# Gate projections with high and low weight columns side by side, and the decay logits of linear attention as one product over stacked rows

## The chip, the cores and the metric

The kernel runs on one core of a Trainium2 chip (trn2). The number that counts is the device time of one execution, in microseconds, taken as the median of several runs. The engines of the core are named as in the profile: PE is the matrix engine (PEld its weight loads), DVE the vector engine, ACT the scalar engine, POOL the GpSimd engine, and SP the queue that starts nearly all DMA transfers.

## The reference

The kernel computes a two-layer encoder over 512 tokens of width 1024, all in float32. Layer 0 mixes tokens by a bidirectional gated delta rule with eight heads (GDN), layer 1 by bidirectional gated linear attention with four heads (GLA). After each mixer there is a squared-ReLU MLP of width 4096, and after each of the four sublayers a residual addition with layer norm. Cut to what the change touches:

```python
# layer 0: beta and decay of each head, from 32 of the projection's columns
proj = jnp.matmul(h, w_in).astype(F32)
ba = proj[..., A_CONV_CH + A_VW:].reshape(bn, s, 2, 2, A_HEADS)
beta = jax.nn.sigmoid(ba[:, :, 0]).transpose(2, 0, 3, 1)
g = (-jnp.exp(a_log) * jax.nn.softplus(ba[:, :, 1] + dt_bias)).transpose(2, 0, 3, 1)

# layer 1: low-rank forget gate, rank 16 in each of the two directions
proj = jnp.matmul(h, w_in).astype(F32)
gl = proj[..., 2 * B_KW + 2 * B_VW:].reshape(bn, s, 2, B_RANK)
gate_logit = jnp.einsum('bsnr,nrk->nbsk', gl, gate_w2) + gate_b[:, None, None, :]
log_a = (jax.nn.log_sigmoid(gate_logit) / B_TAU)
```

In words: layer 0 multiplies the 512 x 1024 activations by 32 extra weight columns and turns the results into `beta` and `g`. Layer 1 multiplies its activations by 32 extra columns too (16 for each direction), and multiplies each 16-wide result by a 16 x 512 matrix `gate_w2[d]`, which gives 128 decay logits for each token, head and direction.

## The kernel before, in words

**Precision.** A float32 product is made of three products in the type `float32r`. Each operand is split into a high part (a copy into a `float32r` tile, on ACT, line 95) and a low part (the difference, on DVE, line 96). `mm3` (lines 111 to 116) then issues three matmuls that add into one PSUM bank: the stationary operand's high part with the moving one's high part (L114), high with low (L115), and low with high (L116). The activations are kept transposed as `xth` and `xtl` (eight blocks of 128 features, 512 tokens).

**Stages.** The order is GDN, MLP, GLA, MLP. Weights are streamed from HBM: each block lands in a ring of three staging buffers (`wst`), is split, and the halves go into rings of three `wh` and three `wl` buffers (`whl`). A staging buffer is free once both halves were made, and a `wh` buffer once the last matmul that reads it is done.

**The start (GdnConst.gates, lines 1080 to 1160).** Twelve idle transposes, then the transposes of token tiles 0 and 1 (`tp`), then `proj_halves` over two products with the 512 tokens in two halves: `bap` (the 32 gate columns) and `pjk` (the first key block). The transposes of tiles 2 and 3 stand between the first `bap` half and the first `pjk` half. After that `bap` is copied to `yr` (32 x 512, ACT, L1112), transposed in four pieces into `gtp` (L1115), and a chain of some twenty DVE operations on 128 x 64 and 128 x 128 tiles (`gy`, `gd`, `gl`) leads to `gy` (L1142), whose cumulative sums are four small products on PE (`gcp`, L1147 and L1148). These PE instructions keep the order in which they are written.

**The start of GLA (gla, lines 670 to 713).** The 32 gate columns are loaded into `gst`, 16 for each direction with a gap of 16 zero columns between (48 columns, so that the directions lie at partitions 0 and 32 of the result). `proj_halves` makes `gps` (48 x 512), `pjq` and `pjk`. `gps` is split into `glh` and `gll`, and `gate_w2` (two DMAs into `w2f`, with zeros between) into `w2h` and `w2l`.

**The decay logits (GlaHead.gates, lines 756 to 773).** For each of four heads and two directions, `mm3` over the 16 rows of that direction gives a bank `lg`: three matmuls with 16 rows and 512 tokens each. Five ACT operations and one DVE addition turn `lg` into the factors `F`. The two calls of head 0 stand in front of the value projection, those of head h+1 in the levels 16 and 32 of head h (line 733), each just before the `scp` product of that level (L851).

**Order.** Within the GLA heads, PE instructions keep the written order (`in_order`, line 708): `behind(n)` puts n pieces of projection work (`pjv`, `pjq`, `pjk`; six matmuls or so each) between the steps of the attention levels. In the rest of the kernel, and on DVE, ACT and SP everywhere, a list scheduler sets the order from its own estimates, so a change of one instruction can move others.

Of the kernel before, what the change touches and what calls it, by code (L numbers as in the profile page):

```python
# [8 lines left out]
F32 = mybir.dt.float32  # L9
F32R = mybir.dt.float32r  # L10
# [3 lines left out]
ALU = mybir.AluOpType  # L14
# [3 lines left out]
P = 128  # L18
S = 512
D = 1024  # L20
KT = D // P
# [7 lines left out]
class Ctx:  # L29
# [97 lines left out]
    def proj_halves(self, specs, between=None):  # L127


        out = [self.bank([P, S], F32, name=name, tag=tag) for _, name, tag in specs]  # L130
        for hf in range(2):
            sl = slice(hf * 256, hf * 256 + 256)
            for ps, ((wh, wl), _, _) in zip(out, specs):
                n = wh.shape[-1]
                for k in range(KT):
                    self.mm3(ps[:n, sl], wh[:, k, :], wl[:, k, :], self.xth[:, k, sl], self.xtl[:, k, sl],
                             k == 0, k == KT - 1)
                if between:
                    between()
                    between = None  # L140
        return out

# [527 lines left out]
def gla(c, gc, w_in, gate_w2, w_out, ln_g, ln_b, w_next):  # L670
# [3 lines left out]
    tc, nc = c.tc, c.nc  # L674
    H = B_H
    with c.banks(ac=2, tp=2, pj=4), tc.tile_pool(name="gla", bufs=2) as pool:
# [3 lines left out]
        gst = c.wst.tile([P, KT, 48], F32, name="gst", tag="wst")  # L680
        nc.vector.memset(gst, 0.0)
        base = 2 * H * P + 2 * H * B_DV
        for d in range(2):
            c.dma(gst[:, :, 32 * d:32 * d + 16], w_in[:, base + 16 * d:base + 16 * d + 16].rearrange("(k p) n -> p k n", p=P))
        gwh, gwl = c.split(gst, [P, KT, 48])
        specs = [((gwh, gwl), "gps", "ac")]
        specs += [(c.wcols(w_in, c0), nm, "pj") for c0, nm in ((0, "pjq"), (H * P, "pjk"))]
        gps, *qk0 = c.proj_halves(specs)
        glh = pool.tile([48, S], F32R, name="glh", tag="glh", bufs=1)
        gll = pool.tile([48, S], F32R, name="gll", tag="gll", bufs=1)  # L690
        nc.scalar.copy(glh, gps[:48, :])
        nc.vector.tensor_tensor(gll, gps[:48, :], glh.bitcast(F32), ALU.subtract)
        w2f = c.wst.tile([48, S], F32, name="w2f", tag="wst")
        nc.vector.memset(w2f, 0.0)
        for d in range(2):
            c.dma(w2f[32 * d:32 * d + 16, :], gate_w2[d])
        w2h = pool.tile([48, S], F32R, name="w2h", tag="w2h", bufs=1)
        w2l = pool.tile([48, S], F32R, name="w2l", tag="w2l", bufs=1)
        nc.scalar.copy(w2h, w2f)
        nc.vector.tensor_tensor(w2l, w2f, w2h.bitcast(F32), ALU.subtract)  # L700

        par = c.load_ln(ln_g, ln_b, lambda i: pool.tile([P, 512], F32, name=f"ln{i}", bufs=1))
        g = (glh, gll, w2h, w2l, gc.gb, gc.ngb, gc.gcol)
# [42 lines left out]
class GlaHead:  # L746
# [9 lines left out]
    def gates(self, d):  # L756

        c, h = self.c, self.h
        V, A = c.nc.vector, c.nc.scalar
        glh, gll, w2h, w2l, gb, ngb, _ = self.consts  # L760
        if d == 0:
            self.F = self.pool.tile([P, 2, S], F32, name="F", tag="F", bufs=2)
        ps = c.bank([P, S], F32, name="lg", tag="tp")
        rows = slice(32 * d, 32 * d + 16)
        c.mm3(ps, w2h[rows, h * P:(h + 1) * P], w2l[rows, h * P:(h + 1) * P], glh[rows, :], gll[rows, :], True, True)
# [4 lines left out]
        r = self.t2("gr", 1)  # L770
# [198 lines left out]
class GdnConst:  # L969
# [110 lines left out]
    def gates(self, st, k0, bia, coef, cw):  # L1080

        c, pool = self.c, self.pool
        nc = c.nc
        G, V = nc.gpsimd, nc.vector
        M = 4 * A_H
# [6 lines left out]
        V.memset(coef[:, :H2], 1.0)  # L1092
        with c.in_order(mybir.EngineType.PE):
# [5 lines left out]
            with self.then():  # L1099
                st = c.split(st, [P, KT, M])  # L1100
                k0 = c.split(k0, [P, KT, P])
# [9 lines left out]
        yr = pool.tile([M, S], F32, name="yr", tag="E", bufs=2)  # L1111
        nc.scalar.copy(yr, ps[:M, :])  # L1112
        tps = c.bank([P, NT, P], F32, name="gtp", tag="tp")
        for n in range(NT):
            nc.tensor.transpose(tps[:, n, :M], yr[:, n * P:(n + 1) * P], c.ident[:M, :M])  # L1115
# [502 lines left out]
```

## Time and profile before

| what | value |
|---|---|
| median of 3 runs | 1383.04 us (1381.99 to 1383.33) |
| span of the profiled execution | 1383.4 us |
| PE busy | 1353.9 us, 98% of the span, 8361 instructions |
| DVE busy | 1073.9 us, 78% |
| ACT busy | 736.6 us, 53% |
| mean granted clock of PE | 0.996 |

The page gives no other time for the profiled execution than its span, from the first to the last instruction; it lies 0.4 us above the median of the runs. Busy times of different engines overlap. A PE matmul is listed with its whole passage through the array, so the distance between two starts, and not the listed duration, is what one matmul costs in a row of them. "Idle before" names what ended the wait of an engine. In a timeline the columns are start, duration, engine, line, operation, output and inputs, tile sizes and count.

### The profile page before, as it was taken

Reading aid. Unit: us, or ns where it says so; the run is one execution under the profiler, and the core shown is the slowest. Engines: PE = TensorE matmul, PEld = TensorE weight load, DVE = VectorE, ACT = ScalarE, POOL = GpSimd, SP = SyncE. Lnnn points to the kernel's source line nnn. Section 1 sums busy time; section 2 is a strip of 40 time slices with the busy share of each in tenths; the row PEclk is TensorE's granted clock in tenths of the full one; section 3 lists DMA queues with packets and bytes.
Section 4 is the critical chain, followed back from the end, with each engine's and each line's share of the span. In section 5 each row is a group of like instructions: output and inputs, shape, how many; then the busy total and the mean of one; then the engine's idle time right before and its main releaser. Section 6 shows DMA issues by size and latency. Waiting matters only on the chain.

```text
span 1383.4 us, 21226 instructions
## 1 busy us (share of the span) xinstructions
PE 1353.9 (98%) x8361; PEld 1130.9 (82%) x8361; DVE 1073.9 (78%) x1682; ACT 736.6 (53%) x1438; POOL 71.8 (5%) x111
## 2 busy tenths in 40 slices
PE   9999999999999999999999999999999999999997
PEld 8777787777777888888887888888878888888876
DVE  6687787778677997887957587866879787979665
ACT  4676568665743655555543354654446455546440
POOL 4000000000003600000000000000000000000000
PEclk9999999999999999999999999999999999999999
DMA  6221112211251523253132322221225153431141
GB/s 177 74 62 47 46 32 62 52 42 32 79 154 56 172 77 109 74 153 92 47 112 75 96 89 62 61 62 61 87 66 177 52 152 92 122 88 50 46 151 47
DMA packets 146122, 117.11 MB, mean 85 GB/s; under 512 B 7632, under 2 KB 122440, under 8 KB 146024
## 3 DMA queue, kind: packets, MB, share of 16 engines
q1 hardware_dynamic: 144679, 111.57, 27.4%
q0 software_dynamic: 1344, 4.20, 1.1%
q8 instruction: 65, 1.06, 0.3%
q14 instruction: 34, 0.27, 0.1%
HBM read 113.66 MB, written 2.10 MB: 84 GB/s over the span
## 4 chain that ended last, share of the span: by engine, by line
PE 86%; ACT 6%; DVE 5%; DMA 2%; issue 1%; POOL 0%; DVEq 0%; ACTq 0%; POOLq 0%
PE pj L115 5%; PE pj L116 5%; PE pj L114 5%; PE pjv L114 3%; PE pjv L115 3%; PE pX L114 3%; PE pjv L116 3%; PE pX L115 3%; PE pX L116 3%; PE scp L851 2%; PE fxz L114 2%; PE op L1544 2%; PE fxz L115 2%; PE fxz L116 2%; DMA wst<-in_mlp_w 2%; PE pl L115 2%
## 5 line engine op out<-in xcount | busy, mean ns | idle before, releaser
L95 ACT CAST wh<-wst 128x1024 fp32r<-128x1024 f32 x146 | 152.9, 1050 | 221.6 <-PE pj L115 50.7
L96 DVE TENSOR_TENSOR wl<-wst,wh 128x1024 fp32r<-128x1024 f32 x146 | 177.8, 1225 | 73.3 <-ACT wh L95 73.1
L115 PE MATMUL pj<-xtl,wh 128*128 128x512 f32 (+1 forms) x352 | 127.9, 363 | 0.5 <-DVE xtl L163 0.5
L114 PE MATMUL pj<-xth,wh 128*128 128x512 f32 (+1 forms) x352 | 127.4, 363 | 0.8 <-ACT xth L162 0.7
L116 PE MATMUL pj<-xth,wl 128*128 128x512 f32 (+1 forms) x352 | 127.4, 362 | 0.0
L96 DVE TENSOR_TENSOR w2l<-w2r,w2h 128x1024 fp32r<-128x1024 f32 x84 | 102.5, 1223 | 26.3 <-ACT w2h L95 26.3
L95 ACT CAST w2h<-w2r 128x1024 fp32r<-128x1024 f32 x84 | 88.2, 1050 | 63.5 <-PE pX L116 28.1
L115 PEld LDWEIGHTS pj<-xtl,wh 128*128 128x128 f32 x352 | 67.2, 191 | 10.9 <-DVE xtl L163 0.8
L114 PEld LDWEIGHTS pj<-xth,wh 128*128 128x128 f32 x352 | 66.9, 191 | 11.2 <-ACT xth L162 1.2
L116 PEld LDWEIGHTS pj<-xth,wl 128*128 128x128 f32 x352 | 67.1, 191 | 10.2
L115 PE MATMUL pX<-w2l,ah 128*128 128x512 f32 x192 | 75.0, 391 | 0.0
L116 PE MATMUL pX<-w2h,al 128*128 128x512 f32 x192 | 74.9, 390 | 0.0
L114 PE MATMUL pX<-w2h,ah 128*128 128x512 f32 x192 | 74.8, 393 | 0.0
L95 ACT CAST ah<-h 128x1024 fp32r<-128x1024 f32 x46 | 48.4, 1053 | 47.1 <-PE pX L115 19.3
L336 DVE TENSOR_TENSOR w2r<-w2r 128x1024 f32<-128x1024 f32 x48 | 57.5, 1222 | 0.3
L96 DVE TENSOR_TENSOR al<-h,ah 128x1024 fp32r<-128x1024 f32 x46 | 56.3, 1223 | 0.6
L114 PE MATMUL pjv<-wh,xth 128*128 128x512 f32 x128 | 54.8, 428 | 0.0
L116 PE MATMUL pjv<-wh,xtl 128*128 128x512 f32 x128 | 50.2, 392 | 0.0
L115 PE MATMUL pjv<-wl,xth 128*128 128x512 f32 x128 | 50.0, 390 | 0.0
L116 PEld LDWEIGHTS pX<-w2h,al 128*128 128x128 f32 x192 | 36.1, 188 | 7.5
L116 PE MATMUL pjk<-xth,wl 128*128 128x512 f32 (+1 forms) x112 | 41.8, 373 | 0.0
L114 PE MATMUL pjk<-xth,wh 128*128 128x512 f32 (+1 forms) x112 | 41.7, 372 | 0.0
(477 smaller groups left out, 3932.0 us busy)
## 6 DMA issues: line engine op xcount, KB each, us to landing
wst<-in_mlp_w SPq DMA_DIRECT2D x80, 512.0 KB, 4.4
w2r<-in_mlp_w SPq DMA_DIRECT2D x48, 512.0 KB, 3.8
wst<-in_a_w_in SPq DMA_DIRECT2D x32, 512.0 KB, 4.1
wst<-in_b_w_in SPq DMA_DIRECT2D x32, 256.0 KB, 3.0
wst<-in_a_w_out SPq DMA_DIRECT2D x8, 512.0 KB, 3.7
wst<-in_b_w_in SPq DMA_DIRECT2D x8, 512.0 KB, 3.8
wst<-in_b_w_out SPq DMA_DIRECT2D x8, 512.0 KB, 3.5
xt<-in_x SPq DMA_DIRECT2D x4, 512.0 KB, 5.3
```

Source lines behind the costliest of these rows:

```text
L95: nc.scalar.copy(hi, src)
L96: nc.vector.tensor_tensor(lo, src, hi.bitcast(F32), ALU.subtract)
L114: mm(ps, ah, bh, start=start, stop=False, **kw)
L115: mm(ps, ah, bl, start=False, stop=False, **kw)
L116: mm(ps, al, bh, start=False, stop=stop, **kw)
L336: V.tensor_tensor(blocks[a + (q,)], blocks[a + (q,)], blocks[b + (q,)], ALU.add)
L851: T.matmul(ps[:, n, :], kh[:, sl], qh[:, sl], start=True, stop=True)
L1544: T.matmul(op[:, n, :], l, r, start=i == 0, stop=i == len(mm) - 1)
```

## The change

**Weights side by side.** A new helper `side_by_side` makes the two halves of a 32-column weight block in one `wh` buffer of 64 columns: for each group of 16 columns, 16 high columns and then the 16 low ones. In place of one cast and one subtraction there are two of each, on 128 x 8 x 16 elements. `proj_halves` takes such a block (with no `wl`) and issues two matmuls for each block of features in place of three: all 64 columns against the high and against the low activations. The results of high and low columns come out on different partitions and have still to be added.

**The start.** `bap` has 64 rows. `yr` is 64 x 512, and the four transposes become four float32 products with `sum2`, a 64 x 32 matrix of zeros and ones that transposes and adds the two rows of each column. `sum2` is made by one DVE addition from the identity matrix.

**GLA.** `gst` has 32 columns, filled by one DMA without zeros. `gps` has 64 rows: for each direction 16 high and 16 low ones. For each direction one tile `glr[d]` of 96 rows is filled from its 32 rows of `gps`: rows 0 to 31 and 64 to 95 get the high part (two ACT copies), rows 32 to 63 the low part (one DVE subtraction). `w2r[d]` is filled by one DMA that reads `gate_w2[d]` six times, so that 96 rows hold it; ACT casts all 96 to the high part, and DVE puts the low part into rows 64 to 95. The decay logits are then one matmul with 96 rows.

```diff
@@ proj_halves @@
                 for k in range(KT):
+                    if wl is None:
+                        self.nc.tensor.matmul(ps[:n, sl], wh[:, k, :], self.xth[:, k, sl], start=k == 0, stop=False)
+                        self.nc.tensor.matmul(ps[:n, sl], wh[:, k, :], self.xtl[:, k, sl], start=False, stop=k == KT - 1)
+                        continue
                     self.mm3(ps[:n, sl], wh[:, k, :], wl[:, k, :], self.xth[:, k, sl], self.xtl[:, k, sl],
                              k == 0, k == KT - 1)
...
+    def side_by_side(self, st, n):
+
+        nc = self.nc
+        w = self.whl.tile([P, KT, n // 16, 2, 16], F32R, name="wh", tag="wh")
+        v = st.rearrange("p k (d r) -> p k d r", r=16)
+        for d in range(n // 16):
+            nc.scalar.copy(w[:, :, d, 0, :], v[:, :, d, :])
+        for d in range(n // 16):
+            nc.vector.tensor_tensor(w[:, :, d, 1, :], v[:, :, d, :], w[:, :, d, 0, :].bitcast(F32), ALU.subtract)
+        return w.rearrange("p k d s r -> p k (d s r)"), None
@@ gla @@
-        gst = c.wst.tile([P, KT, 48], F32, name="gst", tag="wst")
-        nc.vector.memset(gst, 0.0)
+        gst = c.wst.tile([P, KT, 32], F32, name="gst", tag="wst")
         base = 2 * H * P + 2 * H * B_DV
-        for d in range(2):
-            c.dma(gst[:, :, 32 * d:32 * d + 16], w_in[:, base + 16 * d:base + 16 * d + 16].rearrange("(k p) n -> p k n", p=P))
-        gwh, gwl = c.split(gst, [P, KT, 48])
-        specs = [((gwh, gwl), "gps", "ac")]
+        c.dma(gst, w_in[:, base:base + 32].rearrange("(k p) n -> p k n", p=P))
+        specs = [(c.side_by_side(gst, 32), "gps", "ac")]
...
-        glh = pool.tile([48, S], F32R, name="glh", tag="glh", bufs=1)
-        gll = pool.tile([48, S], F32R, name="gll", tag="gll", bufs=1)
-        nc.scalar.copy(glh, gps[:48, :])
-        nc.vector.tensor_tensor(gll, gps[:48, :], glh.bitcast(F32), ALU.subtract)
-        w2f = c.wst.tile([48, S], F32, name="w2f", tag="wst")
-        nc.vector.memset(w2f, 0.0)
+        R = slice(0, 32), slice(32, 64), slice(64, 96)
+        glr, w2r = [], []
         for d in range(2):
-            c.dma(w2f[32 * d:32 * d + 16, :], gate_w2[d])
-        w2h = pool.tile([48, S], F32R, name="w2h", tag="w2h", bufs=1)
-        w2l = pool.tile([48, S], F32R, name="w2l", tag="w2l", bufs=1)
-        nc.scalar.copy(w2h, w2f)
-        nc.vector.tensor_tensor(w2l, w2f, w2h.bitcast(F32), ALU.subtract)
+            w2f = c.wst.tile([96, S], F32, name="w2f", tag="wst")
+            src = gate_w2[d]
+            c.dma(w2f, bass.AP(src.tensor, src.offset, [[0, 6]] + [list(q) for q in src.ap]))
+            t = pool.tile([96, S], F32R, name=f"w2r{d}", bufs=1)
+            nc.scalar.copy(t, w2f)
+            nc.vector.tensor_tensor(t[R[2], :], w2f[R[2], :], t[R[2], :].bitcast(F32), ALU.subtract)
+            w2r.append(t)
+            g = pool.tile([96, S], F32R, name=f"glr{d}", bufs=1)
+            nc.scalar.copy(g[R[0], :], gps[R[d], :])
+            nc.scalar.copy(g[R[2], :], gps[R[d], :])
+            nc.vector.tensor_tensor(g[R[1], :], gps[R[d], :], g[R[0], :].bitcast(F32), ALU.subtract)
+            glr.append(g)
@@ GlaHead.gates @@
-        rows = slice(32 * d, 32 * d + 16)
-        c.mm3(ps, w2h[rows, h * P:(h + 1) * P], w2l[rows, h * P:(h + 1) * P], glh[rows, :], gll[rows, :], True, True)
+        c.nc.tensor.matmul(ps, w2r[d][:, h * P:(h + 1) * P], glr[d], start=True, stop=True)
@@ GdnConst.gates @@
         V.memset(coef[:, :H2], 1.0)
+        self.sum2 = pool.tile([2 * M, M], F32, name="sum2", bufs=1)
+        iv = c.ident[:2 * M, :2 * M].rearrange("p (d s r) -> p d s r", s=2, r=16)
+        V.tensor_tensor(self.sum2.rearrange("p (d r) -> p d r", r=16), iv[:, :, 0, :], iv[:, :, 1, :], ALU.add)
...
-                st = c.split(st, [P, KT, M])
+                st = c.side_by_side(st, M)
...
-        yr = pool.tile([M, S], F32, name="yr", tag="E", bufs=2)
-        nc.scalar.copy(yr, ps[:M, :])
+        yr = pool.tile([2 * M, S], F32, name="yr", tag="E", bufs=2)
+        nc.scalar.copy(yr, ps[:2 * M, :])
         tps = c.bank([P, NT, P], F32, name="gtp", tag="tp")
         for n in range(NT):
-            nc.tensor.transpose(tps[:, n, :M], yr[:, n * P:(n + 1) * P], c.ident[:M, :M])
+            nc.tensor.matmul(tps[:, n, :M], yr[:, n * P:(n + 1) * P], self.sum2, start=True, stop=True)
```

**What moves.** Built, the changed kernel keeps the order of PE but for the matmuls that are gone and for one step: the eight transposes of token tile 2 at the end of the first MLP stand together some eight matmuls earlier than before. On DVE the mask copies of the levels (L885, L887) stand one or two places earlier in each head, some weight subtractions (L96) too, and near the end of the first MLP a clearing of 48 x 512 elements and a weight subtraction are gone from ahead of the last two operations (L216) of tile 2's layer norm. On SP there is one DMA fewer, and the two of `w2f` take two staging buffers where they took one.

More of the change, by code (lines that the diff above doesn't have):

```diff
@@ L702, in gla @@
         par = c.load_ln(ln_g, ln_b, lambda i: pool.tile([P, 512], F32, name=f"ln{i}", bufs=1))
-        g = (glh, gll, w2h, w2l, gc.gb, gc.ngb, gc.gcol)
+        g = (glr, w2r, gc.gb, gc.ngb, gc.gcol)
         heads = [GlaHead(c, pool, h, w_in, g, gc.masks, oth, otl) for h in range(H)]
@@ L759, in gates @@
         V, A = c.nc.vector, c.nc.scalar
-        glh, gll, w2h, w2l, gb, ngb, _ = self.consts
+        glr, w2r, gb, ngb, _ = self.consts
         if d == 0:
```

## The prediction

> **What bounds the kernel now.** I read the page's busy shares first, then the chain of work that ended last, then PE's waits in the two stretches that the diff touches.
>
> ```profile
> PE 1353.9 (98%) x8361; PEld 1130.9 (82%) x8361; DVE 1073.9 (78%) x1682; ACT 736.6 (53%) x1438; POOL 71.8 (5%) x111
> ...
> PE 86%; ACT 6%; DVE 5%; DMA 2%; issue 1%; POOL 0%; DVEq 0%; ACTq 0%; POOLq 0%
> ```
>
> PE is busy for 98% of the span and carries 86% of the chain, so a matmul that goes is worth its step on PE unless a wait takes its place. The waits of PE from 0 to 60 us, from 720 to 960 us, and one stage by engines (duration, then busy time of PE, PEld, DVE, ACT and POOL, granted clock, DMA share, GB/s):
>
> ```profile
> PE gcp L1147 <- DVE gy L1142: 2.3, 1, 2.3
> ...
> PE pjq L114 <- DVE xt L449: 0.9, 1, 0.9
> ...
> 795.00:830.00 35.00, 35.00 (x178) 29.03 (x175) 28.40 (x46) 20.11 (x33) 0.00 (x0) 1.00 0.30 90
> ```
>
> In the GLA heads PE never waits, and DVE works 28.40 of 35 us. At the start PE waits 2.3 us for the chain of gate operations on DVE, so there the end of that chain, not PE, sets the time.
>
> **Six decay-logit calls (heads 1 to 3).** One call with its neighbours, and for comparison a level without such a call:
>
> ```profile
> 824.37 0.39 PE L116 MATMUL pjq<-xth,wl 128*128 128x512 f32 x1
> 824.68 0.50 PE L114 MATMUL lg<-glh,w2h 16*128 16x512 f32 x1
> 825.03 0.40 PE L115 MATMUL lg<-gll,w2h 16*128 16x512 f32 x1
> ...
> 825.59 1.16 PE L851 MATMUL scp<-qh,kh 128*128 128x128 f32 x8
> ...
> 826.82 0.39 PE L115 MATMUL pjq<-xtl,wh 128*128 128x512 f32 x1
> ```
>
> ```profile
> 814.38 0.40 PE L116 MATMUL pjv<-wh,xtl 128*128 128x512 f32 x1
> 814.61 1.05 PE L851 MATMUL scp<-qh,kh 128*128 128x128 f32 x8
> ...
> 815.74 0.40 PE L115 MATMUL pjv<-wl,xth 128*128 128x512 f32 x1
> ```
>
> From the last matmul before to the second one after, the call's stretch takes 826.82 - 824.37 = 2.45 us, the other 815.74 - 814.38 = 1.36 us. Three matmuls of a usual step of 0.23 us (814.38 to 814.61) would be 0.69 us; the call costs 1.09 us. The rest is at the borders: the first `lg` comes after 0.31 us, takes 0.35 us until the next, and from `scp` to the second matmul behind it pass 1.23 us, not 1.13; the third `lg` is left late too. The operand of 16 rows (16*128) is the only thing that differs there. The new matmul has 96 rows, and the built program places it on the array as the 128-row ones; I take it at a usual step of 0.23 us with no border. Gain 1.09 - 0.23 = 0.86 us, six times 5.2 us. From below: if 96 rows have the same borders, the stretch is 0.31 + 0.35 + 1.23 = 1.89 us, and the gain 0.56 us, six times 3.4 us. I take the upper end, as the placing is that of the neighbours.
>
> The Trainium skill ("TensorE: Matmul & The Clock Gate", Part 3, "The mechanism") says that a weight load overlaps running matmuls only where its row group differs. The trace doesn't bear it out in this form: PEld is busy for 29.03 of 35 us under a PE that never waits, nearly all of it loads of 128 rows under matmuls of 128 rows. By that rule 96 rows, which share row groups with 128, would keep the border; that is the first rival below.
>
> **The pair of calls of head 0.**
>
> ```profile
> 794.19 0.28 PE L116 MATMUL pjk<-xth,wl 128*128 128x256 f32 x1
> 794.40 0.50 PE L114 MATMUL lg<-glh,w2h 16*128 16x512 f32 x2
> ...
> 795.30 0.50 PE L114 MATMUL pjv<-wh,xth 128*128 128x512 f32 x1
> 795.63 0.39 PE L115 MATMUL pjv<-wl,xth 128*128 128x512 f32 x1
> ```
>
> Here each row counts two matmuls, one of each direction: the six take 795.30 - 794.40 = 0.90 us, as the three of one call did (825.59 - 824.68 = 0.91 us). The two directions lie on different rows of the array and run side by side, which the change gives up. So the gain is less than twice 0.86 us: 1.44 us (794.19 to 795.63) become 0.12 + 3 x 0.23 = 0.81 us, gain 0.6 us, or with borders 0.21 + 0.35 + 0.23 + 0.33 = 1.12 us, gain 0.3 us.
>
> **The gate columns of GLA (`gps`), and what its products wait for.**
>
> ```profile
> L114 PE MATMUL gps<-xth,wh x16: 276/276/321, 783.2 to 788.3; 128*48 128x256 f32 x16
> ...
> L116 PE MATMUL gps<-xth,wl x16: 276/276/279, 783.4 to 788.6; 128*48 128x256 f32 x16
> ```
>
> The 48 matmuls start between 783.2 and 788.6 us, a step of 5.4 / 47 = 0.115 us. Sixteen go: 1.8 us, all on PE's path, since PE waits for nothing behind them. A load of 64 columns in place of 48 stays under that step. What could be late is the stacked operand of the first `lg`:
>
> ```profile
> 788.76 1.05 ACT L95 CAST wh<-wst 128x1024 fp32r<-128x1024 f32 x1 [6.59 <-PE gps L115]
> 789.71 0.58 ACT L691 CAST glh<-gps 48x512 fp32r<-48x512 f32 x1
> ```
>
> ACT is released by `gps` at 788.76, after the change 1.8 us earlier at 786.9. Then stand two copies of 0.58, the cast of 1.05 and two more copies: 790.3. DVE's last `glr` part follows the 1.2 us subtraction of that cast: about 791.0, estimated. PE reaches `lg` at 794.40 - 1.8 = 792.6, so 1.6 us are left, and the longer chain (three more copies, one more subtraction) costs nothing; without that cover it would cost the excess over 1.6 us once. The two `w2f` DMAs (six times the rows) go out on SP before the `pjv` weights, where before there stood two as well; I cost them at nothing, as they are covered by the 12 us until ACT reads them:
>
> ```profile
> L50 SPq DMA_DIRECT2D w2f<-in_b_gate_w x2: 332/372/413, 767.8 to 768.1; - x2
> ...
> L699 ACT CAST w2h<-w2f x1: 620/620/620, 780.6 to 780.6; 48x512 fp32r<-48x512 f32 x1
> ```
>
> **The moved transposes at the end of the first MLP: a loss.**
>
> ```profile
> 767.21 0.48 DVE L694 MEMSET w2f<- 48x512 f32 x1
> ...
> 767.63 1.21 DVE L96 TENSOR_TENSOR wl<-wst,wh 128x1024 fp32r<-128x1024 f32 x1
> 768.77 1.40 DVE L216 SCALAR_TENSOR_TENSOR xt<-xt,rstd,ln 128x512 f32<-128x512 f32 x2
> ...
> 769.65 0.63 PE L159 MATMUL tp<-ident,xt 128*128 128x128 f32 x4
> ```
>
> The transposes of tile 2 move seven or eight matmuls of 0.23 us forward, to 768.0. DVE's last layer-norm operations lose the clearing and the subtraction ahead of them (768.77 - 767.21 = 1.56 us) but gain about 0.25 us for the second `gst` cast and subtraction: they run from 767.45, end at 768.15 and 768.85, and with the 0.18 us from 769.47 to 769.65 the two groups of four can start at 768.33 and 769.03. PE waits 0.3 and 0.35 us there, less 0.1 us for one change of kind fewer: +0.5 us, between 0 and 0.8.
>
> **The start.**
>
> ```profile
> L114 PE MATMUL bap<-xth,wh x16: 276/276/306, 8.1 to 18.7; 128*32 128x256 f32 x16
> ...
> L116 PE MATMUL bap<-xth,wl x16: 276/276/306, 9.1 to 18.9; 128*32 128x256 f32 x16
> L95 ACT CAST wh<-bst x1: 418/418/418, 7.7 to 7.7; 128x256 fp32r<-128x256 f32 x1
> L95 ACT CAST wh<-gst x1: 513/513/513, 764.7 to 764.7; 128x384 fp32r<-128x384 f32 x1
> 21.95 1.05 ACT L95 CAST wh<-wst 128x1024 fp32r<-128x1024 f32 x1 [1.35 <-PE pjk L115]
> 22.07 0.43 PE L1115 MATMUL gtp<-ident,yr 32*128 32x32 f32 x4
> 22.43 0.50 PE L114 MATMUL pjq<-xth,wh 128*128 128x512 f32 x1
> 23.04 1.32 DVE L96 TENSOR_TENSOR wl<-wst,wh 128x1024 fp32r<-128x1024 f32 x1
> 39.04 0.38 PE L1147 MATMUL gcp<-gy,cum 128*128 128x32 f32 x2 [2.26 <-DVE gy L1142]
> 39.93 0.48 PE L116 MATMUL pjz<-xth,wl 128*128 128x512 f32 x1
> ```
>
> Each half of `bap` loses 8 matmuls. In the second half that is 8 x 0.115 = 0.9 us. In the first, two matmuls now run before the low part is there, and 22 from 9.1 us on: until 11.6. Afterwards all 16 need both parts. A cast of 256 elements takes 418 ns and one of 384 takes 513, so one of 128 some 320 ns, and two 0.23 us more than the one; the subtractions follow behind. I put the start at 9.25 us (9.1 to 9.5) and the end at 9.25 + 16 x 0.115 = 11.1: gain 0.5 us. Four transposes (0.36 us, 22.07 to 22.43) become four float32 products; the nearest row is `gcp`, four such of 32 columns in 39.93 - 39.04 = 0.89 us: +0.5 us. PE is 1.4 us earlier at `gtp` and 0.9 us after it. The DVE chain starts with `gtp` and with the subtraction at 23.04, which waits for the cast at 21.95 and so for `pjk`; they come 0.9 and 1.4 us earlier. I take 1.2 us for the chain's end, and so for the gain, as PE still waits at `gcp` (0.6 to 1.6). The other new instruction, `sum2`, stands on an idle DVE.
>
> **Sum.** -5.2 - 0.6 - 1.8 + 0.5 - 1.2 = -8.3 us against the profiled 1383.4 us, which is 0.4 us over the median of 1383.04. From the median: 1374.7 us.
>
> **Rivals.** First, the borders stay with 96 rows: gains 3.4 and 0.3 in place of 5.2 and 0.6, so 1376.8 us. For it speaks that a row count other than 128 had borders, against it the placing.
>
> Second, the clock drops at the start. After the wait at `gcp` the trace has this stretch (same columns, PE only):
>
> ```profile
> 40.20:43.70 3.50, 3.50 (x10) 0.52 0.36 108
> ```
>
> A wait of 2.26 us and 0.9 us of small products were followed by 3.5 us at half clock, a loss of 1.7 us. The gap of PE ahead of the first `bap` is broken now at 8.1 us; without these two matmuls it lasts some 2.1 us, nearly as long. Then 1374.7 + 1.7 = 1376.4 us; were the drop after `gcp` to go instead, 1373.0. The Trainium skill ("TensorE: Matmul & The Clock Gate", Part 1, "What's actually happening") puts the drop after an idle window of about 3.4 us, free-running. The trace agrees on the 3.4 us at half clock, not on the idle time needed. By the page neither gap would drop the clock.
>
> Third, DVE becomes the bound in the heads: with 28.40 of 35 us busy its share rises as PE shortens, and the six calls' 5.2 us come back as waits: 1379.9 us, and within 0.2% if the pair's and half of `gps`'s go too. PE's lack of any wait there speaks against it.
>
> Fourth, slower: DVE stands earlier in line for the mask copies (L887). If it blocks there until `scp` is done, the E, F, kh and qh work behind it starts late, and the next `scp` waits for kh, with PE's order fixed:
>
> ```profile
> 821.92 0.68 DVE L865 TENSOR_TENSOR kh<-k,E 128x512 f32<-128x512 f32 x1
> ```
>
> A place costs F, kh, qh and a subtraction, 3 x 0.68 + 1.22 = 3.3 us, four heads 13 us: 1388 us. It decides from the point where DVE's lead is gone. This kh is ready at 822.6, 3.0 us ahead of the `scp` at 825.59, and longer ahead of its own one; so I hold it unlikely.
>
> **How the numbers follow.** Forecast 0.60 (own range 1373.5 to 1376.2), borders 0.17, clock 0.10, DVE bound 0.09, slower 0.04. A change under 0.2% (2.8 us) can't be told from none in this kernel; of the DVE rival I count 0.05 as faster and 0.04 as the same. Faster 0.92, same 0.04, slower 0.04. The range goes from 1373.0 (the drop after `gcp` gone) to 1378.5 (borders and a lost 1.7 us), which leaves out the last two rivals.
>
> **What would show it.** `lg` steps of 0.23 us and `scp` 0.23 us behind them confirm 5.2; 0.35 us shows the borders. `gps` should take 3.7 us for 32 starts. `gcp` should start near 37.8 us, `tp` of tile 2 should show waits on L216 of 0.3 us, and the first `bap` start at 9.25. A wait of `lg` on `glr`, of `scp` on kh, or half clock near 10 us would make the prediction wrong.

## The result, and the profile after

The changed kernel takes 1374.01 us in the median of four runs (1370.78 to 1376.46), beside 1383.18 us for the kernel before: ratio 0.9928, 95% interval 0.9913 to 0.9943. Measured once more it was 1373.43 us (six runs) against 1383.12 us: ratio 0.9935, 0.9915 to 0.9955. The forecast was 1374.7 us, with a range from 1373.0 to 1378.5 us. The profiled execution took 1370.78 us, its span is 1369.1 us. That one is 3.2 us faster than the median. In all runs here the span is 1.6 to 2.0 us shorter than the time of its execution, so the profiled execution of before, with its span of 1383.4 us, took about 1385 us, some 2 us over its median and not 0.4. The two spans must not be compared without asking which part of the difference is the change.

The busy shares and the chain of waits of the kernel after:

```profile
PE 1341.5 (98%) x8317; PEld 1123.9 (82%) x8317; DVE 1073.9 (78%) x1685; ACT 738.7 (54%) x1444; POOL 72.5 (5%) x111
...
PE 83%; ACT 7%; DVE 6%; DMA 2%; issue 1%; POOL 0%; DVEq 0%; SPq 0%; ACTq 0%
```

PE is still the bound. It has 44 matmuls fewer; DVE's busy time is the same as before, ACT's 2.1 us longer. PE's waits from 0 to 60 us and from 720 to 960 us (total, times, longest), and the stage that answers to the one from 795 to 830 us:

```profile
PE bap L137 <- DVE wh L155: 2.0, 1, 2.0
...
PE gcp L1164 <- DVE gy L1159: 1.3, 1, 1.3
...
PE scp L865 <- DVE qh L876: 0.7, 1, 0.7
...
789.00:824.00 35.00, 34.33 (x177) 28.98 (x176) 28.90 (x48) 20.76 (x35) 0.00 (x0) 1.00 0.31 90
```

Two things are new: a wait of 2.0 us ahead of `bap`, where before there stood 1.03 and 0.54 us with two matmuls between them, and a wait of 0.67 us of one `scp` in the GLA heads, where PE had waited for nothing. The wait at `gcp` fell from 2.3 to 1.3 us.

**The places of the change.** One decay-logit call with its neighbours, and the pair of head 0 (here one row counts both directions):

```profile
823.18 0.40 PE L116 MATMUL pjk<-xth,wl 128*128 128x512 f32 x1
823.42 0.39 PE L779 MATMUL lg<-glr,w2r 96*128 96x512 f32 x1
823.65 1.05 PE L865 MATMUL scp<-qh,kh 128*128 128x128 f32 x8
...
824.78 0.39 PE L115 MATMUL pjk<-xtl,wh 128*128 128x512 f32 x1
```

```profile
787.46 0.28 PE L116 MATMUL pjk<-xth,wl 128*128 128x256 f32 x1
787.58 0.63 PE L779 MATMUL lg<-glr,w2r 96*128 96x512 f32 x2
...
788.29 0.40 PE L115 MATMUL pjv<-wl,xth 128*128 128x512 f32 x1
```

The stretch takes 824.78 - 823.18 = 1.60 us where it took 2.45: 0.85 us gained, with steps of 0.24 and 0.23 us on both sides of `lg`. The pair takes 788.29 - 787.46 = 0.83 us where it took 1.44: 0.61 us gained. The gate columns, the start, and the moved transposes:

```profile
L137 PE MATMUL gps<-xth,wh x16: 276/276/331, 778.2 to 781.7; 128*64 128x256 f32 x16
L138 PE MATMUL gps<-xtl,wh x16: 276/276/280, 778.4 to 781.8; 128*64 128x256 f32 x16
```

```profile
8.97 0.33 PE L137 MATMUL bap<-xth,wh 128*64 128x256 f32 x1 [2.02 <-DVE wh L155]
...
20.36 1.07 PE L1132 MATMUL gtp<-sum,yr 64*128 64x32 f32 x8
21.37 0.50 PE L114 MATMUL pjq<-xth,wh 128*128 128x512 f32 x1
...
37.05 0.38 PE L1164 MATMUL gcp<-gy,cum 128*128 128x32 f32 x2 [1.34 <-DVE gy L1159]
...
762.59 0.39 PE L116 MATMUL pl<-w2h,w2r 128*128 128x512 f32 x1
762.84 1.29 PE L174 MATMUL tp<-ident,xt 128*128 128x128 f32 x8
```

I compared the starts of PE's matmuls in both traces, in order, and noted where their distance changes:

| place | forecast, us | from trace to trace, us |
|---|---|---|
| start, up to `gcp` | -1.2 | -2.0 (39.04 to 37.05), up to 0.5 of it not the change |
| moved transposes of tile 2 | +0.5 | +0.2, and no wait shown |
| `gps` | -1.8 | -1.7 |
| pair of head 0 | -0.6 | -0.6 |
| `scp` of head 0, second level | none | +0.95 (0.67 us of wait, the rest a border) |
| six calls | -5.2 | -5.1 |
| sum | -8.3 | -8.25 |

Up to 0.5 us of the first row is where the clock rose. In every trace here PE runs at half clock until the first boundary that its clock record shows: ahead of it the transposes follow each other by 0.21 us, behind it, where any are left, by 0.11. In the trace of before it lies at 6.17 us, in that of the changed kernel at 5.09. The kernel with the GLA part alone (below) starts like the one before, and its boundary lies at 4.91 us: its `gcp` starts at 38.55 us, 0.49 us earlier than before with nothing changed ahead of it. Against that trace the changed start gains 1.5 us.

The spans differ by 14.3 us, 6 us more than the sum. Of these, 3.1 us come from the clock: the profiled execution of before spent two periods of 3.41 us at half clock (from 40.31 and from 436.25 us), that of after none. Another 2.4 us were lost near 1331 us by the profiled execution of before alone, where PE waited for late weights:

```profile
PE pl L114 <- ACT w2r L95: 1.4, 1, 1.4
```

None of the other eleven traces of this study has this wait, those with the start or the GLA heads of before among them, so it does not belong to the change. The half clock from 436.25 us comes and goes too: four of the twelve traces have it, among them three with both parts of the change. Whether the one right behind `gcp` is partly the change's is not shown: both traces with the start of before have it, and five of the eight with the changed start and `gcp` in its old place. The change is thus worth 7.8 to 8.3 us in this pair of traces; the medians are 9.2 and 9.7 us apart, with intervals of 8 to 12 and 6 to 12 us.

### The profile page after: what moved, and what is told of

Its sections match the earlier page's. It is cut to its first block, busy times and chain, and to the rows that moved or that the text cites. A ratio compares the mean times of both kernels' runs of the same rounds, so it can differ in the third digit from the quotient of the medians.

```text
span 1369.1 us, 21146 instructions
## 1 busy us (share of the span) xinstructions
PE 1341.5 (98%) x8317; PEld 1123.9 (82%) x8317; DVE 1073.9 (78%) x1685; ACT 738.7 (54%) x1444; POOL 72.5 (5%) x111
## 3 DMA queue, kind: packets, MB, share of 16 engines
q8 instruction: 65, 1.06, 0.3%
## 4 chain that ended last, share of the span: by engine, by line
PE 83%; ACT 7%; DVE 6%; DMA 2%; issue 1%; POOL 0%; DVEq 0%; SPq 0%; ACTq 0%
PE pj L115 5%; PE pj L116 5%; PE pj L114 5%; PE pX L114 3%; PE pX L115 3%; PE pX L116 3%; PE pjv L114 3%; PE pjv L115 3%; PE pjv L116 3%; PE fxz L114 2%; PE scp L865 2%; PE op L1561 2%; PE fxz L115 2%; PE fxz L116 2%; PE pl L115 2%; PE pl L116 2%
## 5 line engine op out<-in xcount | busy, mean ns | idle before, releaser
L96 DVE TENSOR_TENSOR wl<-wst,wh 128x1024 fp32r<-128x1024 f32 x146 | 178.9, 1232 | 62.2 <-ACT wh L95 62.1
L96 DVE TENSOR_TENSOR w2l<-w2r,w2h 128x1024 fp32r<-128x1024 f32 x84 | 102.5, 1222 | 26.6 <-ACT w2h L95 26.5
L96 DVE TENSOR_TENSOR al<-h,ah 128x1024 fp32r<-128x1024 f32 x46 | 56.2, 1221 | 0.6
L114 PEld LDWEIGHTS pX<-w2h,ah 128*128 128x128 f32 x192 | 35.8, 188 | 7.1 <-ACT w2h L95 0.3
```

Of the source, the lines that this page charges most:

```text
L96: nc.vector.tensor_tensor(lo, src, hi.bitcast(F32), ALU.subtract)
L114: mm(ps, ah, bh, start=start, stop=False, **kw)
```

## The experiments

The open questions were whether the six calls' price lies where the forecast put it, what the start is worth once the clock has its say (its gap ahead of `bap` is longer now), and where the new wait of `scp` comes from.

### The start alone, and the GLA part alone

Each kernel takes one part of the diff and leaves the other as before. The first keeps `side_by_side` for `bap`, and `sum2`; the second keeps it for `gps`, and the 96-row product. The first, against the changed kernel:

```diff
-        specs = [(c.side_by_side(gst, 32), "gps", "ac")]
+        gwh, gwl = c.split(gst, [P, KT, 48])
+        specs = [((gwh, gwl), "gps", "ac")]
...
-        c.nc.tensor.matmul(ps, w2r[d][:, h * P:(h + 1) * P], glr[d], start=True, stop=True)
+        c.mm3(ps, w2h[rows, h * P:(h + 1) * P], w2l[rows, h * P:(h + 1) * P], glh[rows, :], gll[rows, :], True, True)
```

> The kernel before with the start alone changed (bap side by side, sum2). Theory, that the gain is the earlier end of the gate chain: gcp starts near 37.05 us as in the changed kernel (39.04 before), all later steps keep their distance, so 2.0 us less: about 1381.2 us; 1.6 us less again where the half clock after gcp stays away. Rival, that the start gives nothing once the clock and the landing of weights are taken out: gcp back at 39 us and 1383.

Measured: 1381.93 us (ten runs) against 1382.51 us, ratio 0.9994 (0.9983 to 1.0005). In its trace `gcp` comes 1.5 us earlier than before, though its clock rose late, at 7.43 us, but the median gains only 0.6 us. The mean granted clock over the ten runs was 0.9953, and 0.9969 over the thirteen runs of the kernel before beside them; 0.0016 of 1380 us is 2.2 us. So the start's gain is real on PE's path, and the clock can have taken most of it. This is argued from means: the one trace of this kernel has no half clock between its start and its last microseconds, and over all 33 runs of the kernel before that list a clock, the mean is 0.9963, not 0.9969.

The second kernel, against the changed one:

```diff
-                st = c.side_by_side(st, M)
+                st = c.split(st, [P, KT, M])
...
-            nc.tensor.matmul(tps[:, n, :M], yr[:, n * P:(n + 1) * P], self.sum2, start=True, stop=True)
+            nc.tensor.transpose(tps[:, n, :M], yr[:, n * P:(n + 1) * P], c.ident[:M, :M])
```

> The kernel before with the GLA part alone changed. Theory: gps 1.7 us less, the pair 0.6 less, six calls 5.1 less, the new wait of scp on qh in head 0 0.9 more: 6.5 us less, about 1376.7 us, whatever the clock does at the start. Rival, that part of the measured gain is the clock alone: the ledger of the starts on PE inside GLA shows under 5 us.

Measured: 1376.04 us (four runs), ratio 0.9952 (0.9934 to 0.9970), 6.5 us less than before. The starts of its matmuls show `gps` -1.7, pair -0.6, `scp` +0.9 and six calls -5.1 us, which is the -6.5 that was expected; the moved transposes, left out there, add 0.2. The gains of the two parts, 0.6 and 6.5 us, come to 7.1 us and not to the 9 us of the whole change; their intervals (0.7 us lost to 2.3 gained for the start, 4 to 9 gained for GLA) are wide enough for the difference.

### Three products in each call, and an operand of 32 rows

If a call before cost two steps of 0.23 us and the borders of a 16-row operand, then three 96-row products should cost two steps more and no border, and one 32-row product a border and no step. The first kernel writes the same product three times into the bank:

```diff
         c.nc.tensor.matmul(ps, w2r[d][:, h * P:(h + 1) * P], glr[d], start=True, stop=True)
+        c.nc.tensor.matmul(ps, w2r[d][:, h * P:(h + 1) * P], glr[d], start=True, stop=True)
+        c.nc.tensor.matmul(ps, w2r[d][:, h * P:(h + 1) * P], glr[d], start=True, stop=True)
```

> The changed kernel with each decay-logit matmul issued three times over 96 rows (the same product again, so the count is that of before, and the result is the same). Theory, that the old call cost three steps and borders, and that 96 rows have no border: a call costs two steps of 0.23 us more than in the changed kernel, 0.46 us, six calls 2.8 us and the pair 0.9. Rival, that the border belongs to three matmuls in a row into one bank: 0.8 us or more a call, 5 us for six.

```profile
821.29 0.40 PE L116 MATMUL pjq<-xth,wl 128*128 128x512 f32 x1
821.52 0.39 PE L779 MATMUL lg<-glr,w2r 96*128 96x512 f32 x1
...
821.99 0.40 PE L781 MATMUL lg<-glr,w2r 96*128 96x512 f32 x1
822.23 1.05 PE L867 MATMUL scp<-qh,kh 128*128 128x128 f32 x8
```

Every step is 0.23 or 0.24 us, and the six calls cost 0.48 us each more than in the changed kernel, the pair 0.9 us. The other kernel leaves out two of the three products, those with the low part of the gate activations and with the low part of `gate_w2`:

```diff
-        c.nc.tensor.matmul(ps, w2r[d][:, h * P:(h + 1) * P], glr[d], start=True, stop=True)
+        c.nc.tensor.matmul(ps, w2r[d][0:32, h * P:(h + 1) * P], glr[d][0:32, :], start=True, stop=True)
```

> The changed kernel with the decay-logit matmul over the first 32 of its 96 rows: the low part of the gate activations and of gate_w2 is left out of the logits. Still one matmul a call. Theory, that the border comes with an operand of fewer than 65 rows or so: the border is back, 0.3 us a call more than with 96 rows, six calls 1.8 us. Rival, that the number of rows does nothing: starts on PE as in the changed kernel within 0.1 us a call.

```profile
822.11 0.39 PE L116 MATMUL pjq<-xth,wl 128*128 128x512 f32 x1
822.43 0.50 PE L779 MATMUL lg<-glr,w2r 32*128 32x512 f32 x1
822.85 1.16 PE L865 MATMUL scp<-qh,kh 128*128 128x128 f32 x8
...
824.08 0.39 PE L115 MATMUL pjq<-xtl,wh 128*128 128x512 f32 x1
```

One product of a third of the rows costs more than one of 96: 0.32 us until it starts and 0.42 us until `scp`, then 1.23 us, together 1.97 us where the changed kernel takes 1.60. From trace to trace each of the six calls costs 0.38 us more. So 0.48 us for two steps and 0.38 us for the border make up the 0.86 us of the forecast, each shown by itself (the border with one product of 32 rows, where the kernel before had three of 16). Where between 32 and 96 rows the border begins, no run shows. The single times (1376.66 and 1377.06 us, one run each) hold half-clock periods and say less than the steps.

The Trainium skill ("TensorE: Matmul & The Clock Gate", Part 3, "The mechanism") has a weight load overlap running matmuls only where its row group differs. These runs don't agree: 96 rows share row groups with the 128-row neighbours and lose nothing, 32 rows lose 0.38 us.

### When the clock drops

The trace records periods of 3.413 us with one clock each. They don't start with the program: the first recorded boundary lay 4.91 to 7.65 us after its first instruction, in another place in each execution. Seven traced executions have the changed start without the ten transposes that follow below. In four of them PE ran at half clock right behind the first `bap`, in three it didn't. Two of them, the changed kernel when measured again and the start alone, with the period that holds the wait and the one behind it (duration, then busy time of PE, PEld, DVE, ACT, POOL, granted clock, DMA share, GB/s):

```profile
7.12:10.53 3.41, 1.56 (x14) 1.33 (x13) 3.04 (x6) 2.41 (x5) 0.00 (x0) 1.00 0.96 345
10.53:13.95 3.42, 3.42 (x19) 3.42 (x18) 0.53 (x2) 0.63 (x2) 0.00 (x0) 0.50 0.71 194
```

```profile
7.43:10.84 3.41, 1.61 (x14) 1.37 (x13) 3.00 (x6) 2.26 (x5) 0.00 (x0) 1.00 0.89 323
10.84:14.26 3.42, 3.42 (x32) 3.42 (x31) 1.70 (x4) 2.16 (x5) 0.00 (x0) 1.00 0.80 219
```

Much the same wait (1.85 and 1.80 us) lay 0.1 us differently in its period: 1.56 us of busy PE were followed by half clock, 1.61 us were not. Over all executions with this start, 1.54 to 1.59 us of work in the period led to half clock (four times), 1.61 us and more to full clock (three times). Around `gcp` there is a boundary too, but elsewhere: up to 2.13 us half clock, 2.17 us and more full clock. At a third place, from 427 to 437 us, periods with up to 1.86 us of work were followed by half clock (four traces), those with 2.06 us and more were not (eight). So the busy time as the profile counts it is not quite what the clock goes by, but within each of the three places it separates every case. In the profile of the changed kernel all three fell on the good side; the start:

```profile
5.09:8.50 3.41, 1.81 (x15) 1.34 (x13) 2.47 (x5) 2.70 (x7) 1.29 (x3) 1.00 1.15 311
```

The Trainium skill ("TensorE: Matmul & The Clock Gate", Part 1, "What's actually happening") describes windows of 3413 ns that run free of the program, and the traces agree. It asks for an idle window before the clock drops, and here the traces differ: 1.56 of 3.41 us, 46% of PE's time, were busy in the first row above, and the clock dropped.

If this is the cause, breaking the gap up should keep the clock:

```diff
             xposes((0, 1), ("ac", "ch", "tp"))
+            for i in range(10):
+                nc.tensor.transpose(idle[:, i % NT, :], c.ident, c.ident)
```

> The changed kernel with ten transposes of the identity (about 0.06 us each) put on TensorE between the transposes of tiles 0 and 1 and the first `bap` product, so that the wait of 1.8 to 2.1 us ahead of `bap` is broken up; nothing of the result changes. Theory (the clock halves for one period of 3.41 us in those executions in which a period falls well on that wait, as at 10.63 us of the kernel with three lg products and at 8.65 us of the one with 32 rows): no half clock near 8 to 14 us, the first `bap` no later than 9.0 to 9.3 us, and the median 1 to 2 us under that of the changed kernel, about 1372.5, ratio 0.992. Rival (the drop at the start has another cause, or is a drop that comes elsewhere later anyway): median that of the changed kernel, about 1374 us, ratio 0.993 to 0.994, and half clock still to be seen in other places as often as before.

```profile
5.16:8.57 3.41, 2.82 (x24) 2.34 (x22) 2.56 (x5) 2.71 (x7) 1.22 (x3) 1.00 1.17 304
```

The period now holds 2.82 us of work, the ten transposes taking 0.11 us each and not 0.06. The clock did what the theory says: none of the three kernels with these transposes has half clock at the start, and over their 15 runs the mean granted clock was 0.9971, against 0.9955 over the 24 runs of all kernels with the changed start and no transposes. The time didn't follow: 1375.58 us (five runs), ratio 0.9945 (0.9927 to 0.9963), not the expected 1372.5. At the same clock as the profiled changed kernel the profiled execution is 1.2 us longer, and the starts of the matmuls put that at one place, at 983 us, where an `stp` product waits for a copy on ACT (0.9 us) that stands behind a weight cast whose data landed late. All three kernels with the transposes have that wait, but so has the GLA part alone, whose start is that of before. Whether the transposes have to do with it stays open.

### The wait of `scp` for qh

In the trace after, this is the place (PE, then ACT, then DVE):

```profile
801.74 1.13 PE L865 MATMUL scp<-qh,kh 128*128 128x128 f32 x8 [0.67 <-DVE qh L876]
```

```profile
794.51 1.04 ACT L95 CAST wh<-wst 128x1024 fp32r<-128x1024 f32 x1
795.44 0.64 ACT L783 ACTIVATE ge<-ge 128x512 f32<-128x512 f32 x1
...
797.44 0.63 ACT L787 ACTIVATE F<-gr 128x512 f32<-128x512 f32 x1 [1.36 <-DVE gr L786]
```

```profile
795.58 1.23 DVE L96 TENSOR_TENSOR wl<-wst,wh 128x1024 fp32r<-128x1024 f32 x1 [2.11 <-ACT wh L95]
...
800.91 0.68 DVE L876 TENSOR_TENSOR qh<-q,F 128x512 f32<-128x512 f32 x1
```

Before, ACT had this order:

```profile
801.37 0.63 ACT L769 ACTIVATE ge<-ge 128x512 f32<-128x512 f32 x1
801.91 1.03 ACT L95 CAST wh<-wst 128x1024 fp32r<-128x1024 f32 x1
802.85 0.63 ACT L773 ACTIVATE F<-gr 128x512 f32<-128x512 f32 x1
```

A weight cast now stands ahead of the last `ge`, between two activations that stood together before. Before, it followed that `ge` and lay over DVE's addition to `gr`, for which F has to wait anyway. Now the addition waits for the later `ge` and stands behind the cast's subtraction on DVE (795.58) as well: from the first `ge` of the pair to F pass 797.44 - 793.99 = 3.45 us, before 802.85 - 800.71 = 2.14. So F is 1.3 us later, and with it the E, F, kh and qh work on DVE. One kernel puts that cast, and its subtraction, behind F:

```diff
-        A.activation(self.F[:, 1 - d, :], r, AF.Exp, scale=-1.0 / 16.0)
+        self.gate = A.activation(self.F[:, 1 - d, :], r, AF.Exp, scale=-1.0 / 16.0)
...
-            wh, wl = c.split(st, [P, 2, 2 * B_DV])
+            with c.tc.issue_after(self.gate.ins) if h == 0 and q == 3 else contextlib.nullcontext():
+                wh, wl = c.split(st, [P, 2, 2 * B_DV])
```

> The changed kernel with the last weight cast of head 0 (the split ahead of `vr`, fourth quarter) held back until the exponential that makes F of the second level has been issued on ScalarE. Theory (the wait of 0.67 us of the first `scp` of the second level for `qh` comes from one ScalarE cast of weights that slipped ahead of `ge` when the logits came earlier): that wait is gone, `scp` starts 0.7 to 0.95 us earlier against the products before it than in the changed kernel, and nothing else moves by over 0.2 us. Rival (VectorE is late there by itself): the wait stays at 0.5 us or more, or goes over to kh or to the products of the fourth quarter.

```profile
804.59 1.06 PE L866 MATMUL scp<-q,ge 128*128 128x128 f32 x8
805.49 1.16 PE L866 MATMUL scp<-qh,kh 128*128 128x128 f32 x8
```

The wait is gone: `scp` follows 0.90 us behind the product before it, not 1.73, and all matmuls behind it come 0.95 us earlier against the changed kernel; nothing else in the GLA heads moves. The cause is the place of this weight split, its cast on ACT and its subtraction on DVE together; the run does not separate the two. The run took 1374.51 us, with three periods at half clock.

### The products over `gy` later, and the edits together

The remaining wait at `gcp` should go if its products stand seven matmuls later in PE's order:

```diff
...
+                    m = c.mm3(ps, wh[:, k, :], wl[:, k, :], c.xth[:, k, :], c.xtl[:, k, :], k == 0, k == KT - 1)
+                    if h == 0 and i == 3 and k == 6:
+                        for s in g.sums:
+                            c.tc.add_manual_dep(s.ins, m.ins.name, mybir.DependencyInfo(
+                                mybir.DependencyClass.NoSync, mybir.DependencyReason.DATA), reason="later")
```

> The changed kernel with the four products over `gy` (lines 1164 and 1165) put seven products of k, v or q later in TensorE's order, so that TensorE no longer waits for VectorE's `gy` there. Theory (the wait of 1.3 us at `gcp` is a plain loss of the start, left over from the 2.3 us of before, and it also gives the clock an occasion to drop): the wait is under 0.2 us, the work behind `gcp` starts about 1.3 us earlier, no half clock between 37 and 47 us; 1.3 us less than the changed kernel at like clock, up to 3 us less where that had dropped. Rival (VectorE is the bound through the first linear attention head and what is gained at `gcp` is waited for again at the first levels): the gain is under 0.4 us from 60 us on.

```profile
PE gcp L1165 <- DVE gy L1159: 0.4, 1, 0.4
```

The wait fell to 0.4 us and PE was 0.8 us better off at 45 us, counted from the first `bap`, which came 0.75 us later in this execution. But the scheduler then set another order for the first GDN heads, new waits of 0.3 us appeared there, and by 425 us 1.5 us had been lost again. One run: 1374.90 us. This is no gain. The three edits together:

> The changed kernel with the three edits of the kernels of this call together: ten transposes ahead of the first `bap`, the weight cast behind F, the products over `gy` seven products later. Theory: the gains add, -0.9 (scp) -1.3 (gcp) -1 to -2 (clock at the start and behind gcp): median about 1370.5 us, ratio 0.991, against about 1374 of the changed kernel. Rival (the scheduler gives part of it back, or the clock's drops move elsewhere): 1372.5 to 1374.

Measured: 1373.16 us (five runs), ratio 0.9932 (0.9916 to 0.9948). The theory's 1370.5 us is missed: of the three gains, that of `scp` came (-0.92 us in the trace) and the clock's (mean 0.9978), the one at `gcp` was given back in the heads, and the `stp` wait took 0.9 us. Without that edit:

> The changed kernel with two of the three edits: ten transposes ahead of the first `bap`, and the weight cast behind F; the products over `gy` stay where the changed kernel has them, because their later place lost 1.5 us in the heads between 60 and 435 us. Theory: against the changed kernel, run beside it on the same chip, 0.95 us less from `scp` and a clock that is higher by 0.001 to 0.002 (1.4 to 2.8 us of time): 2.3 to 3.7 us less, median near 1371.5 where the changed kernel has 1374 to 1375. Rival (transposes that fill the wait only move the drop elsewhere): 0.9 us less at most, mean clock as in the changed kernel.

> The changed kernel itself, unedited, beside the version with two edits and the kernel before on one chip. Theory: ratio 0.993 to 0.9945 to before, mean clock over its runs 0.9955, below the 0.997 of the two kernels with the ten transposes, since the wait ahead of `bap` drops the clock in about half of the executions. Rival: mean clock 0.997, as with the transposes.

Measured on one chip: 1372.51 us (five runs, mean clock 0.9966) for the two edits, 1373.43 us (six runs, 0.9953) for the changed kernel, 1383.12 us for before. The trace of the first shows the `scp` wait gone, but PE waits 1.9 us at `gcp`, 0.6 us longer than in the changed kernel (the reason stands below, at the start), and 0.6 us at `stp`. The version with the two edits is 0.9 us faster in the median, not the 2.3 to 3.7 us of its theory, and its interval (0.9918 to 0.9943) does not separate it from the changed kernel (0.9915 to 0.9955). The ratio and the clock expected for the changed kernel came true. A better kernel than the changed one is thus not shown, and the clock's drops are only part of what spreads its runs.

## Why the prediction was right, and where it was not

The forecast lay 0.7 us over the first median and 1.3 us over the second, and the sum of its steps agrees with the traces to 0.05 us. That closeness is in part luck: three errors cancel, and up to 0.5 us of the measured sum is not the change.

**Six calls, pair, `gps`: right, with their reasons.** 5.1, 0.6 and 1.7 us against 5.2, 0.6 and 1.8. The choice between 96 rows with and without a border, which carried 1.8 us, was made by the placing; the products of 32 and of three times 96 rows confirm it. The first rival (borders stay) is out. `glr` was ready in time, as said: `lg` waits for nothing. That a load of 64 columns stays under the 0.115 us step of `gps` holds for the step, which is 0.116 us after; the load itself is listed with 0.13 us.

**The start: mis-sized, 1.2 where the traces have 1.5 to 2.0.** Two bounds in it were off but small: `bap` starts at 8.97 and not 9.25 us, and the four products cost 21.37 - 20.36 = 1.01 us in place of 0.36, so 0.65 more and not 0.5. The step that failed is "they come 0.9 and 1.4 us earlier. I take 1.2 us for the chain's end". The chain's parts did come 1.06 and 1.29 us earlier, but the chain itself also became shorter, and that wasn't looked for. DVE and POOL, before:

```profile
24.28 1.31 DVE L1131 TENSOR_SCALAR gd<-ge 128x128 f32<-128x128 f32 x1
...
27.08 1.14 DVE L1133 TENSOR_TENSOR ge<-ge,gd 128x128 f32<-128x128 f32 x1
```

```profile
23.44 2.07 POOL L1059 TENSOR_TENSOR off<-blk 128x512 f16<-128x512 f32 x1
...
26.78 1.29 POOL L1059 TENSOR_TENSOR off<-blk 128x512 f16<-128x512 f32 x1
```

And after:

```profile
21.75 2.35 DVE L96 TENSOR_TENSOR wl<-wst,wh 128x1024 fp32r<-128x1024 f32 x1
24.03 0.36 DVE L1148 TENSOR_SCALAR gd<-ge 128x128 f32<-128x128 f32 x1
...
25.86 0.37 DVE L1150 TENSOR_TENSOR ge<-ge,gd 128x128 f32<-128x128 f32 x1
```

```profile
21.73 1.29 POOL L1073 TENSOR_TENSOR off<-blk 128x512 f16<-128x512 f32 x1
```

The same two operations take 1.31 and 1.14 us where they meet POOL's TENSOR_TENSOR, and 0.36 and 0.37 us where they don't. Before, both met it; after, POOL starts first, the weight subtraction meets it (2.35 us, not 1.32), and both operations are free: 0.95 + 0.77 - 1.03 = 0.69 us, which is what 1.29 lacks to 2.0. Against the GLA part alone, whose clock rose about as early as in the changed kernel, the subtraction starts 0.9 us earlier (22.65 to 21.75) and the chain is 0.6 us shorter, which makes the 1.5 us. This part of the gain isn't firm. The kernel with the later cast, whose edit lies 770 us behind, has the other outcome:

```profile
23.81 1.22 DVE L96 TENSOR_TENSOR wl<-wst,wh 128x1024 fp32r<-128x1024 f32 x1
24.95 1.32 DVE L1149 TENSOR_SCALAR gd<-ge 128x128 f32<-128x128 f32 x1
```

```profile
23.80 2.38 POOL L1074 TENSOR_TENSOR off<-blk 128x512 f16<-128x512 f32 x1
```

Here it is POOL's operation that is held up, DVE's gate operations meet it afterwards, and PE waits 1.9 us at `gcp`, not 1.3. The two engines start within 0.02 us of each other in both kernels, with POOL listed first in both, so the listed starts don't tell which of them will be held up. Six of the ten traces with the changed start show the first outcome, four the second. Those four are just the kernels with an edit of the order, which speaks for the build and against chance; what in the build decides is open. The Trainium skill ("SBUF — State Buffer", "SBUF: two separate sides") tells of a port pair that DVE and GpSimd share under an exclusive lock: whichever operation starts first keeps it to its end, and the other is blocked, not slowed. The rows agree that one of the two is held up by about the other's length, DVE in the one case (2.35 us for 1.22) and POOL in the other (2.38 us for 1.29). That the first one keeps it they don't show: in the second case POOL is listed 0.01 us ahead and is the one held up.

**The clock: the second rival, and it happens in a part of the executions.** It was held at 0.10 as an alternative. The traces show it as a coin toss: half clock behind the first `bap` in four of seven. Half clock near 10 us was one of the prediction's own signs of being wrong; the profiled execution of the changed kernel doesn't show it, but the one of the same kernel measured again does. It can account for most of what the start lost (the start alone: 0.6 us in the median), and its opposite, no drop behind `gcp`, is what makes the profiled execution 1.6 us better there. The rival's reason was right, that a gap of some 2 us is enough; that the phase of the periods decides was missed.

**The moved transposes: +0.5 forecast, +0.2 measured.** The step "PE waits 0.3 and 0.35 us there" didn't come true. The eight transposes follow the matmul ahead of them by 0.25 us without a listed wait.

**Not foreseen: +0.95 us at `scp`.** The fourth rival asked whether DVE's lead could vanish and measured that lead in one level of a later head, 3.0 us. In head 0 it was about 0.5 us before already: the `scp` of the second level started at 808.12 us, and its qh was made from 806.93 to 807.60.

```profile
806.93 0.67 DVE L862 TENSOR_TENSOR qh<-q,F 128x512 f32<-128x512 f32 x1
```

The logits came earlier against the weights there, and a weight cast came one operation earlier in ACT's order. It was not the mask copies, and not four heads but one.

The third rival (DVE becomes the bound) is out: DVE is busy for 28.90 of 35 us, 0.50 us more than before, and PE waits at that one place only.

## What to carry to other kernels

A matmul with few rows between matmuls of 128 rows is dearer than its size says: here 0.38 us of border for 32 rows and none for 96, so that stacking the products of a split along the rows won twice. Before a short wait of PE is made longer, even by taking out work that broke it up, ask what is left in a window of 3.4 us: a gap of 2 us can cost 1.7 us more in a part of the executions, and no single profile shows that. Two traces of a start can be compared only if the clock rose at about the same time in both. And the slack behind a reordering has to be read at the tightest place, the first head here, not at a typical one.

## What the hardware showed that I had not expected

- The clock halves after periods in which PE was busy for 1.59 of 3.41 us, and not after 1.61 us at the same place; at two other places of the kernel the boundary lies between 2.13 and 2.17 us and between 1.86 and 2.06 us.
- Until the first boundary on record, 4.91 to 7.65 us after the first instruction, PE works at half clock (transposes 0.21 us apart, then 0.11). In the ten traces with the changed start the first `bap` began between 8.81 and 9.72 us; it came later with a later boundary, to within 0.05 us.
- DVE operations of 0.36 us took 1.31 and 1.14 us beside a TENSOR_TENSOR of POOL. Whether they or a weight subtraction are hit makes 0.6 us of PE's wait at `gcp`, and starts within 0.02 us of each other stand ahead of both outcomes.
- Four float32 products of 64 rows and 32 columns took 1.01 us, four transposes in their place 0.36 us; the trace lists eight matmuls for the four products.
